# Two key and bias buffers in attention, four-token gate one-hots and another hand-over order in a hybrid transformer block

## The chip, the cores and the metric

The kernel runs on one core of one Trainium2 chip. The metric is device time in microseconds of one launch. The profiled execution is one further launch with the hardware profiler on.

## The reference

One layer on x of 1024 tokens by 1024 features, in f32:

```
mod = silu(c) @ w_ada + b_ada                  # shift, scale, gate for both halves
h = rms_norm(x) * (1 + scale1) + shift1
proj = h @ w_in
  heads A (8 x 64): attention of each 64-token chunk on itself and 8 chunks before it,
                    q and k normed, a learned bias by clipped distance, softmax
  heads B (4 x 128): short causal conv on q, k, v, then the chunked gated delta rule
x = x + gate1 * (concat(A, B) @ w_out)
h2 = rms_norm(x) * (1 + scale2) + shift2
PEER: q = h2 @ w_query; for each of 8 heads top 16 of 128 x 128 product keys
      y = sum_k gate_k * gelu(u_k . h2) * v_k   # u, v rows of expert_down, expert_up (16384 x 1024)
out = x + gate2 * y
```

## The kernel before, in words

The tokens are 8 tiles of 128 and are worked on in the groups [0], [1, 2], [3, 4], [5, 6], [7]. All work up to the expert stage is written as generators, each called under a lane name (lines 1056 to 1074):

- P, `project` (lines 395 to 507): norm, all input projections of a group; the results go to the DRAM tensor `rec` by kind and tile.
- D, `delta` (589 to 664): the delta rule of one tile, with a state that goes from tile to tile. Its tiles come from a ring of 12 buffers of 128 x 512 f32.
- M, `attention` (510 to 569): one tile, one head pair after the other (four pairs). For a pair, `kv` (line 516) receives the queries (line 517) and five tiles of keys and of values (line 519), and `near` (line 521) the bias of the two nearest tiles. Scores (line 532) go to PSUM, VectorE adds the bias and takes the extreme (line 536), ScalarE takes the exponential (539), TensorE transposes (548) and multiplies with the values (556). `kv` and `near` have one buffer each and the lane has one PSUM bank.
- O, `output` (688 to 755): output projection, residual, second norm and the query product with its top 16, for a group.
- R, `choose` (767 to 846): the top 16 of the candidates and the softmax weights of a tile.
- G, `gates_dense` (851 to 885), for tiles 2 to 5: it spreads the 128 weights of each token over the 128 x 128 experts. For 8 tokens at a time (`GQ`, line 66), VectorE makes two one-hot tiles of 128 x 1024 in f16 (line 870); for each token ScalarE scales the second of them twice, by a high and a low part (line 877), and TensorE multiplies it with the first (line 878). Four tokens fill a PSUM bank, which ScalarE empties into `stg` (line 881); 16 tokens of `stg` are stored to `gd`. The one-hot and scaled tiles come from a ring of six buffers, and the lane has one PSUM bank, that of R.

Tiles 0, 1, 6 and 7 take the sparse path instead: `down` and `up` (894 to 930) gather 128 rows of 4 KB per token slot through GpSimd's queue, and VectorE works on them. Those of tile 0 and the down part of tile 1 are issued in the front; the others stand beside the dense stage. The dense stage (932 to 1031) runs tiles 2 to 5 against all 16384 experts; its buffers take the place of those of the lanes, which are released ahead of it (line 1075).

The order of the instructions on each engine is fixed when the program is built. A planner runs through all of them and, on each engine, takes the ready instruction with the lowest priority number; a buffer is taken when one of its ring is free. The numbers come from the lane and the tile alone: `when` (line 1053) gives tile number x 10000 plus the lane's constant in `PRI`, `lane` (line 141) sets it, and each instruction counts it on. So for tile t, delta rule and attention come before output, projections of later tiles and gates:

```
PRI = {'P': -2000, 'D': -15000, 'M': -16000, 'O': -5000, 'R': 0, 'G': 5000, 'A': 60000, 'U': 59000, 'C': 2000000}
```

PSUM tiles of a lane come from its own banks (`BANKS`: P 2, D 2, M 1, O 2, R 1), unless `SPREAD` names several lanes for a tile; then `mm` (line 151) takes their banks in turn.

Of the kernel before, what the change touches and what calls it, by code (L numbers as in the profile page):

```python
# [30 lines left out]
P = 128  # L31
# [17 lines left out]
NROW = 3  # L49
NMORE = 4  # L50
NHELD = 2
RINGS = {'P': 4, 'D': 12, 'M': 4, 'O': 3, 'R': 2, 'G': 6}
XBUFS = {'P': 1, 'O': 2}
WBUFS = {'P': 4, 'O': 3}
STEP = 10000
PRI = {'P': -2000, 'D': -15000, 'M': -16000, 'O': -5000, 'R': 0, 'G': 5000, 'A': 60000, 'U': 59000, 'C': 2000000}
SPREAD = {('P', 0): 'PR', ('D', 0): 'DDO'}
LAYOUT = 'acc more upp rawp wd dn hc gp'
DBUFS = dict(acc=1, more=NMORE, wd=SCN + 1, upp=SCN, hc=1, gp=3, dn=2, rawp=3)
FIRST = {'P': 1000, 'D': 1000, 'M': 1000, 'O': 1000, 'R': 1000, 'G': 1000}  # L60
# [2 lines left out]
SHIFT = {}  # L63
SLOPE = {}
BANKS = dict(P=2, D=2, M=1, O=2, R=1)
GQ = 8
GROUPS = [[0], [1, 2], [3, 4], [5, 6], [7]]
STARTS = [0, 16, 24] + [32 + 4 * k for k in range(5)] + [52 + k for k in range(8)]
LEVELS = (1, 2, 4, 8, 16, 32, 64)
# [49 lines left out]
def hybrid_layer(ctx, tc, a, out):  # L119
# [36 lines left out]
    def lt(shape, dt, name, bufs, tag=None):  # L156
        return pools_[cur[0][0]].tile(list(shape), dt, name=name, tag=(tag or name) + cur[0], bufs=bufs)
# [352 lines left out]
    def attention(t, mixT):  # L510
        m0 = max(0, 4 - t)
        nk = 5 - m0
        oa = rg()
        for p in range(4):
            cs = slice(p * P, (p + 1) * P)
            kv = lt([P, 11, P], F, "kv", 1)
            SP.dma_start(kv[:, 0, :], rec[QA, t][:, cs])
            for n, kind in ((1, KA), (6, VA)):
                SP.dma_start(kv[:, n + m0:n + 5, :],
                             rec[kind, t - 4 + m0:t + 1, :, cs].rearrange("m p c -> p m c"))  # L520
            near = lt([P, 2, 256], F, "near", 1)
            SP.dma_start(near, neard[:, 2 * p:2 * p + 2])
            ss_, rs = [], sm(2)
            for hh in range(2):
                hp = slice(hh * 64, hh * 64 + 64)
                s = lt([P, 640], F, "sx", 2)
                init = BIG
                for lo, hi, bias in ((m0, 3, farm[:, min(m0, 2) * P:]), (max(m0, 3), 5, near[:, hh, (max(m0, 3) - 3) * P:])):
                    if lo >= hi:
                        continue  # L530
                    ps = mm()
                    PE.matmul(ps[:, :(hi - lo) * P], kv[hp, 0, :],
                              kv[hp, 1 + lo:1 + hi, :].rearrange("p m c -> p (m c)"), start=True, stop=True,
                              skip_group_check=True)
                    mf = sm(1)
                    V.tensor_tensor_reduce(s[:, lo * P:hi * P], ps[:, :(hi - lo) * P], bias, -1.0, init, OP.add,
                                           OP.min, accum_out=mf)
                    init = mf
                A_.activation(s[:, m0 * P:], s[:, m0 * P:], AF.Exp, bias=mf, scale=-1.0, accum_out=rs[:, hh:hh + 1])
                ss_.append(s)  # L540
            yield
            blocks = [(hh, m) for hh in range(2) for m in range(m0, 5)]
            PT = {}
            for b0 in range(0, len(blocks), 4):
                part = blocks[b0:b0 + 4]
                pt = mm()
                for n, (hh, m) in enumerate(part):
                    PE.transpose(pt[:, n * P:(n + 1) * P], ss_[hh][:, m * P:(m + 1) * P], ident)
                d = rg()
                A_.activation(d[:, :len(part) * P], pt[:, :len(part) * P], AF.Copy)  # L550
                for n, bm in enumerate(part):
                    PT[bm] = d[:, n * P:(n + 1) * P]
            po = mm()
            for hh in range(2):
                for m in range(m0, 5):
                    PE.matmul(po[:, hh * 64:hh * 64 + 64], PT[hh, m], kv[:, 6 + m, hh * 64:hh * 64 + 64],
                              start=(m == m0), stop=(m == 4), skip_group_check=True)
            V.reciprocal(rs, rs)
            V.tensor_tensor(v3(oa[:, cs], 2), v3(po[:, 0:P], 2), b3(rs, AD), OP.mult)
            yield  # L560
        junk = rg()
        ss = sm(1)
        A_.activation(junk, oa, AF.Square, accum_out=ss)
        r = rsqrt(ss, 1, 1.0 / 512)
        A_.activation(oa, oa, AF.Copy, scale=r)
        ps = transpose4(oa)
        for j in range(4):
            A_.activation(mixT[:, j, :], ps[:, j * P:(j + 1) * P], AF.Copy, scale=mixg[:, j:j + 1])
        yield
# [281 lines left out]
    def gates_dense(t):  # L851
# [11 lines left out]
        V.tensor_tensor(parts[:, 1, :], parts[:, 0, :], ghalf, OP.subtract)  # L863
        for blk in range(8):
            stg = lt([P, P, 16], F, "stg", 1)
            for q in range(2):
                n0 = blk * 16 + q * GQ
                oh1, oh2, whi, wlo = (rg((P, GQ * P), BF).rearrange("p (n i) -> p n i", n=GQ) for _ in range(4))
                for oh, key in ((oh1, 0), (oh2, 1)):
# [184 lines left out]
        return max(FIRST.get(name, 1000), t * SLOPE.get(name, STEP) + PRI[name] + SHIFT.get((name, t), 0))  # L1054

    tc.cur_priority = 0
    for n, g in enumerate(GROUPS):
        lane("P", when("P", g[0]), run, project(g), tile_=g[0])
        if n == 0:
            with tc.issue_after(first_loads):  # L1060
                lane("M", NEARP, run, near_bias())
            lane("P", ADAP, run, ada_rest())
        mixT = pools_["O"].tile([P, KD, 256], F, name="mixT", tag="mixT", bufs=1)
        for tt, t in enumerate(g):
            own = mixT[:, :, tt * P:(tt + 1) * P]
# [29 lines left out]
```

## Time and profile before

| what | value |
|---|---|
| runs | 3506.4, 3490.28, 3504.95 us; median 3504.95 us |
| profiled execution | 3495.83 us, span of its instructions 3494.1 us |
| mean granted TensorE clock | 0.902 |
| TensorE busy (matmul) | 3014.0 us, 86% |
| VectorE busy | 2719.5 us, 78% |
| ScalarE busy | 1316.2 us, 38% |
| GpSimd busy | 1310.2 us, 37% |
| HBM | 282 GB/s over the span |

Shares are of the span of the profiled execution. PE is TensorE, DVE VectorE, ACT ScalarE, POOL GpSimd, SP the engine whose queue issues nearly all other transfers. A row such as "DVE x <- PE y" is idle time of the first engine that a signal of the second ended. Since the kernel has two parts with different work, the averages over the span say little; the stretches have to be read one by one.

### The profile page before, as it was taken

Reading aid. Unit: us, or ns where it says so; the run is one execution under the profiler, and the core shown is the slowest. Engines: PE = TensorE matmul, PEld = TensorE weight load, DVE = VectorE, ACT = ScalarE, POOL = GpSimd, SP = SyncE. Lnnn points to the kernel's source line nnn. Section 1 sums busy time; section 2 is a strip of 40 time slices with the busy share of each in tenths; the row PEclk is TensorE's granted clock in tenths of the full one; section 3 lists DMA queues with packets and bytes.
Section 4 is the critical chain, followed back from the end, with each engine's and each line's share of the span. In section 5 each row is a group of like instructions: output and inputs, shape, how many; then the busy total and the mean of one; then the engine's idle time right before and its main releaser. Section 6 shows DMA issues by size and latency. Waiting matters only on the chain.

```text
span 3494.1 us, 44943 instructions
## 1 busy us (share of the span) xinstructions
PE 3014.0 (86%) x15196; PEld 2482.1 (71%) x15196; DVE 2719.5 (78%) x6407; ACT 1316.2 (38%) x2833; POOL 1310.2 (37%) x1028
## 2 busy tenths in 40 slices
PE   7988868798887898576877699999999999999998
PEld 5677756677766787465756577877777777777777
DVE  3347668768899778993585888988888888889898
ACT  2333134233235663386767632222222222222222
POOL 0000333432333323430000155556655556655563
PEclk9988878899878899686878899999999999999999
DMA  8865888898777987773435699999999999999997
GB/s 283 284 215 174 274 282 267 270 336 280 261 250 230 354 297 261 258 250 125 157 119 176 218 345 334 344 341 339 328 330 336 344 337 349 335 333 355 344 332 283
DMA packets 375959, 989.71 MB, mean 283 GB/s; under 512 B 33440, under 2 KB 139296, under 8 KB 375728
## 3 DMA queue, kind: packets, MB, share of 16 engines
q0 software_dynamic: 147456, 536.94, 43.4%
q1 hardware_dynamic: 228272, 449.90, 37.6%
q8 instruction: 119, 1.95, 0.2%
q14 instruction: 112, 0.92, 0.1%
HBM read 924.84 MB, written 61.87 MB: 282 GB/s over the span
## 4 chain that ended last, share of the span: by engine, by line
PE 37%; DMA 26%; DVE 20%; issue 9%; ACT 5%; POOL 3%; SPq 0%; DVEq 0%; POOLq 0%; ACTq 0%
PE at L982 12%; DMA row<-in_peer_expert_down_dram,idx 8%; PE yk L1005 6%; PE mm L365 5%; PE yc L1005 4%; DVE row L903 4%; DMA row<-in_peer_expert_up_dram,idx 4%; DMA rawu<-in_peer_expert_up_dram 4%; DVE y L920 4%; PE mm L351 3%; DMA rawd<-_peer_expert_down_t_dram 2%; POOL row L901 2%; DMA g<-gd 2%; ACT rg L877 2%; DMA w<-in_w_ada_dram 1%
## 5 line engine op out<-in xcount | busy, mean ns | idle before, releaser
L901 POOL DMA_INDIRECT row<-in_peer_expert_down_dram,idx x512 | 645.5, 1261 | 1113.0 <-DVE s L310 353.7
L915 POOL DMA_INDIRECT row<-in_peer_expert_up_dram,idx x512 | 664.5, 1298 | 1035.5 <-DMA g<-gd 421.3
L903 DVE CUSTOM_DVE_ANT_0 row<-row,h2a 128x1024 f32<-128x1024 f32 x512 | 619.7, 1222 | 139.4 <-DMA row<-in_peer_expert_down_dram,idx 138.6
L920 DVE SCALAR_TENSOR_TENSOR y<-row,act,y 128x1024 f32<-128x1024 f32 x508 | 651.8, 1283 | 53.3 <-DMA row<-in_peer_expert_up_dram,idx 50.1
L877 ACT ACTIVATE rg<-rg,gparts 128x128 f16<-128x128 f16 x1024 | 318.3, 396 | 75.7 <-PE mm L878 49.0
L985 ACT ACTIVATE gl<-at 128x512 f32<-128x512 f32 x128 | 76.4, 597 | 670.8 <-PE at L982 670.8
L982 PE MATMUL at<-hhi,dhi 128*128 128x512 f32 x1024 | 260.6, 396 | 16.3 <-ACT dhi L963 16.2
L365 PE MATMUL mm<-h2T,w 128*128 128x256 f32 (+1 forms) x1280 | 251.8, 358 | 19.0 <-DMA w<-in_peer_w_query_dram 8.2
L982 PE MATMUL at<-hlo,dhi 128*128 128x512 f32 x1024 | 256.8, 392 | 0.0
L1005 PE MATMUL yk<-uhi,whi 128*128 128x512 f32 x512 | 202.5, 412 | 61.7 <-ACT whi L991 56.4
L351 PE MATMUL mm<-w,hT 128*128 128x256 f32 x1024 | 249.3, 398 | 7.3 <-DMA w<-in_w_in_dram 4.6
L982 PE MATMUL at<-hhi,dlo 128*128 128x512 f32 x1024 | 254.7, 389 | 0.7 <-DVE dlo L964 0.7
L365 PEld LDWEIGHTS mm<-h2T,w 128*128 128x128 f32 x1280 | 218.2, 205 | 44.7 <-DMA w<-in_peer_w_query_dram 9.7
L982 PEld LDWEIGHTS at<-hhi,dhi 128*128 128x128 f32 x1024 | 194.7, 191 | 60.1 <-ACT dhi L963 19.0
L351 PEld LDWEIGHTS mm<-w,hT 128*128 128x128 f32 x1024 | 199.2, 200 | 45.3 <-DMA w<-in_w_in_dram 6.4
L982 PEld LDWEIGHTS at<-hlo,dhi 128*128 128x128 f32 x1024 | 194.4, 190 | 41.0
L982 PEld LDWEIGHTS at<-hhi,dlo 128*128 128x128 f32 x1024 | 192.2, 188 | 41.0 <-DVE dlo L964 1.2
L1005 PE MATMUL yk<-ulo,whi 128*128 128x512 f32 x512 | 204.0, 404 | 3.5 <-DVE ulo L964 3.5
L1005 PE MATMUL yc<-uhi,whi 128*128 128x512 f32 x512 | 205.1, 401 | 0.5 <-DVE yacc L1014 0.5
L1005 PE MATMUL yc<-ulo,whi 128*128 128x512 f32 x512 | 204.2, 399 | 0.0
L1005 PE MATMUL yc<-uhi,wlo 128*128 128x512 f32 x512 | 199.5, 390 | 0.0
L870 DVE TENSOR_TENSOR rg<-iota_n,gkeys 128x1024 f16<-128x1024 f16 x128 | 151.0, 1222 | 55.9 <-PE mm L878 55.8
(300 smaller groups left out, 5582.1 us busy)
## 6 DMA issues: line engine op xcount, KB each, us to landing
w<-in_w_in_dram SPq DMA_DIRECT2D x140, 512.0 KB
rawd<-_peer_expert_down_t_dram SPq DMA_DIRECT2D x128, 512.0 KB
rawu<-in_peer_expert_up_dram SPq DMA_DIRECT2D x128, 512.0 KB
w<-in_peer_w_query_dram SPq DMA_DIRECT2D x80, 512.0 KB
gd<-stg SPq DMA_DIRECT2D x64, 512.0 KB
g<-gd SPq DMA_DIRECT2D x32, 1024.0 KB
w<-in_w_ada_dram SPq DMA_DIRECT2D x48, 512.0 KB
w<-in_w_out_dram SPq DMA_DIRECT2D x40, 512.0 KB
```

The source lines that it names most:

```text
L351: PE.matmul(ps[t][:, hf * 256:hf * 256 + 256], hT[:, k, tt * P:(tt + 1) * P], w[k], start=(k == 0), stop=(k == KD - 1), skip_group_check=True)
L365: PE.matmul(ps[:, (c % per) * W:(c % per + 1) * W], w[k][:, (c % 2) * P:(c % 2 + 1) * P], hT[:, k, :W], start=(k == 0), stop=(k == KD - 1) ...
L870: V.tensor_tensor(oh, iota_n[:, None, :].to_broadcast([P, GQ, P]), keys[:, key, n0:n0 + GQ, None].to_broadcast([P, GQ, P]), OP.is_equal)
L877: A_.activation(w[:, n, :], oh2[:, n, :], AF.Copy, scale=parts[:, m, n0 + n:n0 + n + 1])
L901: G.indirect_dma_start(out=r, out_offset=None, in_=a["peer_expert_down"], in_offset=bass.IndirectOffsetOnAxis(ap=idx[:, j:j + 1], axis=0))
L903: V.tensor_tensor_reduce(r, r, h2, 1.0, 0.0, OP.mult, OP.add, accum_out=act[:, j:j + 1])
L915: G.indirect_dma_start(out=row, out_offset=None, in_=a["peer_expert_up"], in_offset=bass.IndirectOffsetOnAxis(ap=idx[:, j:j + 1], axis=0))
L920: V.scalar_tensor_tensor(y, row, w[:, j:j + 1], y, op0=OP.mult, op1=OP.add)
L982: PE.matmul(ps, l[:, k, :], r[:, k, :], start=(n == 0), stop=(n == 3 * KD - 1))
L985: A_.activation(g, ps, AF.Gelu)
L1005: PE.matmul(ps, l[:, ts_], r[:, cs], start=(m == 0 and (s == 0 or not own)), stop=(m == 3 * SCN - 1 and (s == NK // SCN - 1 or not own)))
```

## The change

Five edits. `kv` and `near` of attention get two buffers each. The gates work on 4 tokens at a time, so that a one-hot tile is 128 x 512 and there are four quarters in a block of 16 tokens in place of two halves. The delta rule's ring has 11 buffers. Tile 5's gates take PSUM banks of lanes G (one) and P (two) in turn. The projections of group n + 1 are handed over before the delta rule, attention, output and routing of group n, instead of after them.

```diff
-RINGS = {'P': 4, 'D': 12, 'M': 4, 'O': 3, 'R': 2, 'G': 6}
+RINGS = {'P': 4, 'D': 11, 'M': 4, 'O': 3, 'R': 2, 'G': 6}
...
-SPREAD = {('P', 0): 'PR', ('D', 0): 'DDO'}
+SPREAD = {('P', 0): 'PR', ('D', 0): 'DDO', ('G', 5): 'GP'}
...
-GQ = 8
+GQ = 4
...
-            kv = lt([P, 11, P], F, "kv", 1)
+            kv = lt([P, 11, P], F, "kv", 2)
...
-            near = lt([P, 2, 256], F, "near", 1)
+            near = lt([P, 2, 256], F, "near", 2)
...
-            for q in range(2):
+            for q in range(16 // GQ):
...
-    for n, g in enumerate(GROUPS):
+    def projections(n):
+        g = GROUPS[n]
         lane("P", when("P", g[0]), run, project(g), tile_=g[0])
         if n == 0:
             with tc.issue_after(first_loads):
                 lane("M", NEARP, run, near_bias())
             lane("P", ADAP, run, ada_rest())
+
+    projections(0)
+    for n, g in enumerate(GROUPS):
+        if n + 1 < len(GROUPS):
+            projections(n + 1)
         mixT = pools_["O"].tile([P, KD, 256], F, name="mixT", tag="mixT", bufs=1)
```

## Rows read from the trace of the kernel before

**Rows 1.** The page, TensorE's busy tenths and granted clock in 40 slices of the span.

```profile
PE   7988868798887898576877699999999999999998
PEclk9988878899878899686878899999999999999999
```

**Rows 2.** Busy time by stretch: start:end, length, engines, granted clock, DMA share, GB/s.

```profile
0.00:1965.00 1965.00, 1576.46 (x9042) 1311.04 (x9043) 1387.51 (x4671) 904.57 (x2308) 440.99 (x394) 0.85 0.72 244
1965.00:3494.00 1529.00, 1437.55 (x6157) 1171.08 (x6155) 1332.03 (x1737) 411.63 (x527) 869.17 (x634) 0.98 0.93 334
1200.00:1580.00 380.00, 293.00 (x1807) 249.68 (x1805) 328.28 (x1116) 215.51 (x572) 126.57 (x106) 0.84 0.80 271
1580.00:1640.00 60.00, 35.27 (x170) 25.43 (x171) 23.78 (x58) 42.73 (x126) 0.00 (x0) 0.51 0.33 108
1640.00:1838.00 198.00, 164.96 (x936) 135.55 (x935) 130.01 (x621) 134.62 (x394) 0.00 (x0) 0.81 0.42 140
```

**Rows 3.** Timeline of TensorE where the dense stage begins: start us, us, line, operation.

```profile
1936.90 0.44 PE L365 MATMUL mm<-h2T,w 128*128 128x128 f32 x2
...
1964.50 1.01 PE L878 MATMUL mm<-rg 128*128 128x128 f16 x8 [2.48 <-ACT stg L881]
1967.20 3.55 PE L982 MATMUL at<-hhi,dhi 128*128 128x512 f32 x8 [1.69 <-ACT dhi L963]
```

**Rows 4.** Ends of lanes by line (first and last start), and one from ScalarE's timeline.

```profile
L568 ACT ACTIVATE mixT<-mm,mix_gain x32: 347/361/386, 182.7 to 1837.6; 128x128 f32<-128x128 f32 x32
...
1638.51 1.11 ACT L568 ACTIVATE mixT<-mm,mix_gain 128x128 f32<-128x128 f32 x4
...
L663 ACT ACTIVATE mixT<-mm,mix_gain x8: 687/687/738, 180.2 to 1666.7; 128x512 f32<-128x512 f32 x8
...
L837 DVE TENSOR_TENSOR gd<-gd,s x4: 277/296/303, 1051.6 to 1811.8; 128x128 f32<-128x128 f32 x4
...
L881 ACT ACTIVATE stg<-mm x32: 575/597/620, 1635.7 to 1803.6; 128x512 f32<-128x512 f32 x32
...
L858 DVE CAST gkeys<-mm x4: 417/426/427, 1090.1 to 1822.2; 128x256 f16<-128x256 f32 x4
```

**Rows 5.** Timeline of TensorE, first and last seam between two head pairs of attention.

```profile
1217.64 1.91 PE L556 MATMUL mm<-kv,rg 128*128 128x64 f32 x8
...
1231.36 0.91 PE L532 MATMUL mm<-kv 64*128 64x384 f32 x2
...
1791.75 2.13 PE L556 MATMUL mm<-kv,rg 128*128 128x64 f32 x9
...
1797.80 1.62 PE L532 MATMUL mm<-kv 64*128 64x384 f32 x2 [1.37 <-DMA kv<-rec]
```

**Rows 6.** Waits of SP's queue in the front: us, times, longest.

```profile
SPq L517 <- PE mm L556: 127.7, 26, 13.1
...
SPq L522 <- DVE s L536: 93.2, 21, 20.0
```

**Rows 7.** VectorE's groups in the front: count, busy us, mean ns, idle before.

```profile
L870 DVE TENSOR_TENSOR rg<-iota_n,gkeys 128x1024 f16<-128x1024 f16 x128 | 151.0, 1222 | 55.9 <-PE mm L878 55.8
...
L632 DVE TENSOR_TENSOR rg<-rg,mm 128x512 f32<-128x512 f32 x40 | 27.3, 683 | 11.0 <-PE mm L630 10.9
...
L820 DVE TENSOR_TENSOR rg<-rg 128x512 f16<-128x512 f16 x28 | 11.3, 426 | 0.0
```

**Rows 8.** Waits from 1461 to 1975 us, gates of tiles 3 to 5.

```profile
DVE rg L870 <- PE mm L878: 50.5, 20, 7.6
...
ACT rg L877 <- PE mm L878: 31.7, 19, 4.9
...
ACT rg L877 <- DVE rg L870: 20.0, 7, 5.8
```

**Rows 9.** Waits from 1822 to 1975 us, gates of tile 5.

```profile
PE mm L878 <- ACT stg L881: 30.3, 12, 6.4
...
DVE rg L870 <- PE mm L878: 25.2, 7, 7.6
```

## The prediction

> **What bounds the kernel now.** I read the page's slices first: TensorE's digits are 9s only in the second part of the span, and in the first part both they and the granted clock are uneven [rows 1]. The table by stretches puts numbers to it: up to 1965 us (the front: projections, delta rule, attention, output, routing, gates) TensorE is busy 1576 of 1965 us at a granted 0.85, from there to the end (the dense expert stage) 1438 of 1529 us at 0.98 [rows 2]. The diff touches nothing in the dense stage, so I leave its 1529 us alone and ask only when it can start. The timeline around 1965 us shows that: tile 7's last query matmuls end at 1937, tile 5's gates still run at 1965 and the first dense matmul starts at 1967 [rows 3]. Two chains thus reach the same point: output of tile 7, which needs attention of tile 7, and gates of tile 5, which need output and routing of group [5, 6].
>
> The ends of the lanes say which lane is behind both. Attention of tile 7 ends at 1838 while the delta rule of that tile has been done since 1667; attention of tile 6 ends at 1639, the output of [5, 6] starts there, routing of tile 5 is done at 1812, and tile 5's gate keys are taken at 1822, after the last evacuation of tile 4's gates at 1804 [rows 4]. So attention is the late lane, by 170 us over the delta rule, and the gate lane comes second.
>
> **Attention's second buffers.** The tile `kv` holds queries, keys and values of one head pair, and with one buffer the loads of the next pair cannot be issued until the last value matmul of this one. From tile 5's second pair to tile 7's fourth there are eleven such seams. From the end of the last value matmul to the next first score matmul they last 11.8 us (the first, 1219.6 to 1231.4), then 17.3, 15.4, 48.1, 5.3, 8.8, 3.8, 21.9, 4.1, 9.7 and 3.9 us (the last, 1793.9 to 1797.8) [rows 5]: 150.1 us in all, 110.5 us in the seven ahead of the output of [5, 6]. The queue that issues the loads shows the same from its side: SP stood 127.7 us, 26 times, in front of the query load for the value matmul, and 93.2 us in front of `near` for the pass over the scores [rows 6]. Both waits go; the 128 loads of attention (32 of queries, 64 of keys and values, 32 of `near`) then stand earlier in SP's order than the weight loads that queued behind them. What they come to wait for next is the projection's stores of keys and values, unchanged by the diff.
>
> How much of 110.5 us is gained? Not all: TensorE did other lanes' work in the seams. From 1200 to 1838 us it was busy 293.0 + 35.3 + 165.0 = 493.3 of 638 us, so 22.7% idle [rows 2]. If only idle time can be filled, the gain is 0.227 x 110.5 = 25 us; if attention simply goes first and the other work finds room elsewhere, 110 us (150 us for tile 7's chain). Work of attention has to be finished before output, routing and gates can be, while most of what ran in the seams does not, so I take half, **55 us**, and keep 25 and 150 for the range.
>
> **Gate one-hots of four tokens.** The 128 VectorE operations of 1024 columns become 256 of 512; ScalarE's and TensorE's counts stay, with as many evacuations and stores. The price of a 512-column operation on this operand is not in the trace. The present one takes 1222 ns for 1024, one element a cycle as for f32; an f32 operation of 512 columns takes 683 ns, the 16-bit fold of 512 columns in routing 426 ns [rows 7]. I take the f32 row, since both it and the present form run at the slow rate: 256 x 0.683 - 151.0 = 24 us more VectorE time over four tiles. By the fold's row it would be 42 us less, which is the other end. The Trainium skill (VectorE: DVE Perf Modes, The perf-mode tier table) says that a 16-bit `tensor_tensor` in SBUF runs at twice the rate; that is the fold's price, and the sum would be 42 us less VectorE time. The trace does not bear it out for this operation, whose 1222 ns is the single rate, one operand being a key repeated along the columns. VectorE was busy 130.0 of 198 us from 1640 to 1838 us [rows 2], so this is covered where ScalarE has one-hots in hand; ScalarE waited for them 20.0 us from 1461 us to the end of the front [rows 8]. I charge a quarter of that, **+5 us**.
>
> The ring keeps six buffers, now of half the size, and a quarter still needs four. So the point where ScalarE's second scaled one-hot must wait for TensorE's last matmul of the quarter before comes every four tokens instead of every eight. ScalarE waited so 31.7 us from 1461 to 1975 us [rows 8]; doubled that is +32 us, and 0 if each wait halves. I take a third, **+11 us**. VectorE's own wait in that ring, 50.5 us, should come twice as often and half as long; I take 0, with -25 and +50 as ends.
>
> **Three banks for tile 5's gates.** In that tile's stretch TensorE waited 30.3 us for ScalarE to empty the one bank, and VectorE 25.2 us for those matmuls to give ring buffers back [rows 9]. With three banks in turn, two of them left idle by the projections, a block's matmuls no longer wait for the evacuation before. At most 30 us, at least 0 (ScalarE's own work for a block remains and may set the pace alone); I take half, **-15 us**.
>
> **The rest at nothing.** The delta rule's ring goes from 12 to 11 buffers: a load or a transpose waits for the next free one. Its cover is the 170 us by which this lane is ahead at tile 7 [rows 4]; if attention gained all 150 us, that cover would shrink to 20 us. Handing the next group's projections over first changes no priority number: `when` works it out from lane and tile, and `where` carries it on, whatever the order of the calls. I count 0, and no more than a few us either way from ties. It adds no DMA and moves none past POOL's.
>
> **Sum.** -55 + 5 + 11 - 15 = -54 us. The profiled execution took 3495.83 us (span 3494.1), so 3442 us. The median of the runs shown is 9.1 us above it, where the same saving reads 3451; I give 3446.
>
> **Rivals.** First, **one bank keeps attention in series**: the lane's PSUM bank (M=1) is not doubled, and every score, transpose and value product of a pair passes through it. Then the second `kv` saves only what the load itself takes, while the gates' +16 and -15 us cancel. For it: the eleven seams are 150 of the 618 us from the first of them to the end of tile 7's attention; three quarters of a pair's time lie inside the pair, where the bank is held. Against it: SP's 127.7 us were waits for the buffer, not the bank. Time about 3496, within 0.5% of before (I call 17 us, 0.5% of the median, the least that a measurement of this kernel can tell from no change). The Trainium skill (Perfetto Trace Analysis, Matmuls) asks that independent groups rotate through several banks; by it the gates' change pays and attention's does not.
>
> Second, **the gate ring decides**, on the slow side: gates of tiles 3, 4 and 5 follow one another from 1461 to 1974 us, so this lane too reaches the end of the front. If both ring waits double (+31.7 and +50.5 us), with +5 for the one-hots, and attention yields only its 25 us, no bank gain left, the result is 3495.8 + 62 = 3558 us; with half the doubling it is 3495.8 + 41 + 5 - 25 = 3517 us. It decides as soon as the ring's growth passes what attention and banks give, 25 to 70 us. For it: VectorE's 50.5 us is the longest wait on an engine there that serves every lane. Against it: a half-size quarter also frees its buffers in half the time.
>
> Third, **all seams close**: -150 + 1 = 3347 us, with the other work moved into TensorE's idle time and its clock higher for it. For it: the front's granted 0.85 beside 0.98 later [rows 2]. Against: VectorE was 86% busy from 1200 to 1580 us, which attention needs too.
>
> **How the numbers follow.** The forecast, attention's seams closing in part, gets 0.53, with its own range 3380 to 3487. All seams 0.12, one bank 0.17, the gate ring 0.18. Faster by over 0.5% (under 3487): 0.53 + 0.12 = 0.65; within 0.5%: 0.17; slower: 0.18. The range runs from 3360 to 3530: it leaves out most of the third rival and the upper half of the second.
>
> **What would show it.** In the profile after: SP's waits for the value matmul and for `near` gone or below a third; seams of 2 to 4 us; attention of tile 7 ending some 50 us before 1838, the first dense matmul near 1913, and the dense stage still 1529 us long. The one-hot operations should be 256 of about 0.68 us, and TensorE's wait for the evacuation in tile 5's stretch below 15 us. I am wrong if attention ends where it did (bank), if gates of tiles 3 and 4 take over 170 us each (ring), if the dense stage changes its length by more than 15 us, or if the delta rule ends behind attention.

## The result, and the profile after

The changed kernel takes 3470.75 us (median of 6 runs, 3465.62 to 3477.73), the kernel before 3501.63 us in the same session (6 runs); the ratio is 0.9927 with the 95% interval 0.9902 to 0.9952. So it is faster by 31 us by the medians and by 26 us by the ratio, where 59 were forecast (3504.95 for the kernel before, 3446 for the changed one). Two runs below had one slow execution each (4358.66 us at a granted clock of 0.63, 5008.53 at 0.55), and their medians are of the five others. The profiled execution of the changed kernel took 3471.64 us with a span of 3469.9.

The page's slices, TensorE's busy tenths and granted clock, against [rows 1]:

```profile
PE   7887788799888998688967999998999999999998
PEclk9998878899878998688958999999999999999999
```

The nines begin one slice earlier than in [rows 1], and an 8 stands among them where there was none. The table by stretches (start:end, length, TensorE, weight loads, VectorE, ScalarE, GpSimd, granted clock, DMA share, GB/s) gives the sizes, against [rows 2]:

```profile
0.00:1923.00 1923.00, 1580.15 (x9053) 1297.53 (x9054) 1407.43 (x4844) 912.08 (x2314) 421.15 (x394) 0.86 0.73 250
1923.00:3469.90 1546.90, 1442.78 (x6144) 1174.80 (x6144) 1319.37 (x1693) 407.26 (x517) 873.06 (x634) 0.97 0.91 329
1574.00:1777.00 203.00, 168.06 (x998) 138.75 (x998) 140.45 (x653) 157.17 (x458) 0.00 (x0) 0.81 0.42 147
```

The front holds the same TensorE work (1580 us busy, 1576 before) in 42 us less. The dense stage has 18 us more, at 329 instead of 334 GB/s and a clock 0.01 lower. From the first dense matmul (1922.7, 1967.2 before) to the end of the span it is 1547 us long instead of 1527. So the front gives 44 us and the dense stage takes 20 back. These are one profiled execution each. In the three later runs that change the kernel before behind its front alone, the first dense matmul is at 1952 to 1979; in the five that do so to the changed kernel, at 1920 to 1931.

TensorE's timeline where the dense stage begins, against [rows 3], now runs from tile 5's last gate matmul straight into it:

```profile
1921.47 0.58 PE L878 MATMUL mm<-rg 128*128 128x128 f16 x2 [0.48 <-ACT rg L877]
1922.74 3.47 PE L982 MATMUL at<-hhi,dhi 128*128 128x512 f32 x8 [0.69 <-ACT stg L881]
```

The ends of the lanes (shortest, median and longest ns, first and last start), against [rows 4]:

```profile
L568 ACT ACTIVATE mixT<-mm,mix_gain x32: 348/368/379, 177.7 to 1778.1; 128x128 f32<-128x128 f32 x32
L663 ACT ACTIVATE mixT<-mm,mix_gain x8: 680/687/703, 181.5 to 1604.7; 128x512 f32<-128x512 f32 x8
L837 DVE TENSOR_TENSOR gd<-gd,s x4: 279/282/283, 1030.6 to 1751.6; 128x128 f32<-128x128 f32 x4
L858 DVE CAST gkeys<-mm x4: 407/417/426, 1065.1 to 1788.0; 128x256 f16<-128x256 f32 x4
```

Attention ends 59.5 us earlier (1837.6 to 1778.1), the delta rule 62, routing of tile 5 60, and tile 5's gates begin 34 us earlier. All lanes moved together, and attention stayed the late one.

The first seam of [rows 5], at tile 5's second head pair, now reads:

```profile
1195.00 4.32 PE L556 MATMUL mm<-kv,rg 128*128 128x64 f32 x20
1201.82 1.02 PE L532 MATMUL mm<-kv 64*128 64x384 f32 x2
```

The seam is 2.5 us (11.8 before). Of the eleven, nine are 2.5, 3.8, 6.8, 3.5, 2.4, 12.1, 1.3, 8.8 and 1.3 us, 42.5 in all where they were 80.1. The two at the start of a tile stay, 43.5 us (48.1) and 23.1 us (21.9): there attention waits for something other than the buffer. Half of the gain came earlier than I had counted: tile 5's second pair starts 30 us earlier already (1201.8, 1231.4 before). SP's waits of the front, against [rows 6], did not go and did not fall below a third:

```profile
SPq L517 <- PE mm L556: 103.0, 20, 13.9
...
SPq L522 <- DVE s L536: 51.9, 13, 18.4
```

SP still waits, since two pairs are loaded ahead and the third stands where the second stood; but the wait now lies a pair ahead of its use.

The gates. VectorE's one-hots as the page groups them (busy us, mean ns, idle before), against [rows 7]; then the waits from 1455 to 1925 us against [rows 8], and of tile 5's gates alone, 1788 to 1925 us, against [rows 9]:

```profile
L870 DVE TENSOR_TENSOR rg<-iota_n,gkeys 128x512 f16<-128x512 f16 x256 | 164.9, 685 | 74.8 <-PE mm L878 69.3
```

```profile
DVE rg L870 <- PE mm L878: 58.3, 26, 8.3
ACT rg L877 <- PE mm L878: 39.7, 22, 6.6
...
ACT rg L877 <- DVE rg L870: 23.6, 26, 3.2
```

```profile
DVE rg L870 <- PE mm L878: 28.5, 12, 5.5
PE mm L878 <- ACT rg L877: 18.5, 23, 2.7
PE mm L878 <- ACT stg L881: 4.3, 2, 3.0
```

256 one-hots of 685 ns (683 forecast); the ring's two waits grew by 7.8 and 8.0 us; TensorE's wait for the evacuation fell from 30.3 to 4.3 us, and in its place it waits 18.5 us for ScalarE's one-hots. From the cast of a tile's keys (L858) to the end of its last evacuation (L881), the gates of tiles 3, 4 and 5 take 184, 154 and 135 us, where they took 165, 177 and 152: tile 3 is over the 170 that the forecast named as the sign of the ring, tile 4 is not, and the sum falls.

Last the dense stage, which the forecast did not look at. TensorE's waits there, in the kernel before from 1965 us and in the changed one from 1923 us (us, times, longest; `at` is the first product with the expert weights, `yk` the second):

```profile
PE yk L1005 <- ACT whi L991: 56.4, 27, 5.2
PE at L982 <- ACT dhi L963: 16.2, 7, 3.4
PE yk L1005 <- ACT uhi L963: 5.0, 3, 2.1
```

```profile
PE yk L1005 <- ACT whi L991: 60.2, 23, 5.3
PE at L982 <- ACT dhi L963: 30.9, 9, 6.7
PE yk L1005 <- ACT uhi L963: 2.3, 5, 1.2
```

All gaps between the stage's matmuls add up to 81 us before and 95 after, and the matmuls themselves take 1437 and 1443 us for the same work. These 14 + 6 are the 20 us. TensorE is the busiest engine of this stage and waits for ScalarE, which splits the expert weights (`dhi`) and the gated tile (`whi`) into two parts.

### The profile page after: what moved, and what is told of

Its sections match the earlier page's. It is cut to its first block, busy times and chain, and to the rows that moved or that the text cites. A ratio compares the mean times of both kernels' runs of the same rounds, so it can differ in the third digit from the quotient of the medians.

```text
span 3469.9 us, 45183 instructions
## 1 busy us (share of the span) xinstructions
PE 3022.9 (87%) x15196; PEld 2472.3 (71%) x15196; DVE 2726.8 (79%) x6535; ACT 1319.3 (38%) x2830; POOL 1294.2 (37%) x1028
## 4 chain that ended last, share of the span: by engine, by line
PE 26%; issue 8%; DMA 7%; POOL 5%; DVE 5%; ACT 3%; POOLq 0%; ACTq 0%; SPq 0%; DVEq 0%
PE at L982 11%; PE yk L1005 5%; PE yc L1005 4%; POOL row L915 3%; DMA rawu<-in_peer_expert_up_dram 3%; POOL row L901 2%; PE mm L365 2%; DMA rawd<-_peer_expert_down_t_dram 2%; ACT rg L877 1%; PE mm L351 1%; DVE row L903 1%; DVE rg L870 1%; DMA row<-in_peer_expert_up_dram,idx 1%; DMA row<-in_peer_expert_down_dram,idx 1%; DMA gd<-stg 1%
## 5 line engine op out<-in xcount | busy, mean ns | idle before, releaser
L915 POOL DMA_INDIRECT row<-in_peer_expert_up_dram,idx x512 | 652.3, 1274 | 1085.0 <-issue 431.1
L877 ACT ACTIVATE rg<-rg,gparts 128x128 f16<-128x128 f16 x1024 | 329.5, 395 | 105.7 <-PE mm L878 57.0
L365 PEld LDWEIGHTS mm<-h2T,w 128*128 128x128 f32 x1280 | 211.1, 198 | 31.4 <-DMA w<-in_peer_w_query_dram 8.4
L870 DVE TENSOR_TENSOR rg<-iota_n,gkeys 128x512 f16<-128x512 f16 x256 | 164.9, 685 | 74.8 <-PE mm L878 69.3
```

The costliest lines, as they stand in the source:

```text
L365: PE.matmul(ps[:, (c % per) * W:(c % per + 1) * W], w[k][:, (c % 2) * P:(c % 2 + 1) * P], hT[:, k, :W], start=(k == 0), stop=(k == KD - 1) ...
L870: V.tensor_tensor(oh, iota_n[:, None, :].to_broadcast([P, GQ, P]), keys[:, key, n0:n0 + GQ, None].to_broadcast([P, GQ, P]), OP.is_equal)
L877: A_.activation(w[:, n, :], oh2[:, n, :], AF.Copy, scale=parts[:, m, n0 + n:n0 + n + 1])
L915: G.indirect_dma_start(out=row, out_offset=None, in_=a["peer_expert_up"], in_offset=bass.IndirectOffsetOnAxis(ap=idx[:, j:j + 1], axis=0))
```

## Experiments

All are compared with runs of the kernel before on the same chip; medians and ratios with 95% intervals. "Gaps" are TensorE's between the first dense matmul and the last, from the profiled execution.

**Four parts of the change.** The hand-over alone, put into the kernel before, leaves every engine's instructions in the same order, so it was not run; two pairs of key and bias buffers without four-token one-hots do not fit in SBUF, nor does the delta rule's ring of 12 beside them, so neither was run alone.

```
-            kv = lt([P, 11, P], F, "kv", 2)
-            near = lt([P, 2, 256], F, "near", 2)
+            kv = lt([P, 11, P], F, "kv", 1)
+            near = lt([P, 2, 256], F, "near", 1)
```

> The changed kernel with one buffer each for kv and near again; the four-token one-hots, the 11-buffer ring, the hand-over order and tile 5's three banks stay. Theory A (the gain of the front is attention's seams): attention of tile 7 ends again at 1825 to 1850 us, the first dense matmul comes at 1955 to 1975, and the time is 3490 to 3515 us. Rival B (the gain is the gates' three banks): the first dense matmul stays at 1925 to 1940 and the time at 3470 to 3485 us.

Measured: 3480.41 us, 0.9961 (0.9940 to 0.9982). Attention ends at 1823.6 and the first dense matmul is at 1956, 33 us after that of the changed kernel, yet only 10 us of this show in the time, which lies under the 3490 to 3515 us that were expected: gaps 70 us instead of 95. The second pair does what it should in front, and the dense stage hides it.

```
-SPREAD = {('P', 0): 'PR', ('D', 0): 'DDO', ('G', 5): 'GP'}
+SPREAD = {('P', 0): 'PR', ('D', 0): 'DDO'}
```

> The changed kernel with tile 5's gates on the one bank of their lane again; all else stays. Theory A: attention of tile 7 still ends near 1777 us, TensorE waits 25 to 35 us for the evacuation in tile 5's stretch, the first dense matmul comes 5 to 20 us later than 1923. Rival B: 30 us or more later. Apart from that the dense stage is asked: if its 1547 us in the changed kernel (1527 before) come from the order in which the gathers of the sparse tiles are interleaved there, which this edit puts back to the pattern of before, it lasts 1520 to 1530 us here and the total is about 3470; if they come from the one-hots, the ring or an earlier start, it lasts 1540 to 1550.

Measured: 3458.62 us, 0.9879 (0.9851 to 0.9907), 12 us faster than the changed kernel. But tile 5's gates are slower with the one bank: they take 147 us instead of 135, their last evacuation is at 1949 instead of 1922 (15 of these 27 us are there when their keys come, at 1803 instead of 1788), and expert tile 8, counted from 0, starts at 2024 instead of 2003. The first dense matmul is at 1920, 3 us earlier and not 5 to 20 later as expected: the stage starts while the gates still run. TensorE's wait for the evacuation in these gates (1802 to 1950 us) is back at 25 us:

```profile
PE mm L878 <- ACT stg L881: 25.0, 15, 4.1
```

So with the banks expert tile 8 comes 20 us earlier, 12 of them in tile 5's gates, and the dense stage takes more than that away again: 1323 us from expert tile 8 to tile 120 here, 1359 in the changed kernel, 1329 in the kernel before. (From the first dense matmul to the end it is 1538 us, neither of the two lengths that were expected.) From here on the question was what makes this stretch longer.

```
-    projections(0)
     for n, g in enumerate(GROUPS):
-        if n + 1 < len(GROUPS):
-            projections(n + 1)
+        projections(n)
```

> The changed kernel with the projections handed over in the old order, group by group. Theory C (the order of the calls matters only where two lanes share banks: tile 7's projections then come behind tile 5's gates in the projections' two banks): tile 7's projections end later than 1600 us instead of 1542, attention of tile 7 ends 30 us or more later than 1777, and the time is 3500 us or more. Rival D (priority numbers alone decide, as the prediction has it): the same time as the changed kernel, 3465 to 3480 us.

Measured: 3637.42 us, 1.0404 (1.0378 to 1.0430). The step that I priced at nothing is worth 167 us here. The last of the projections' decay line (L432), of the gates' keys (L858) and of attention (L568), first and last start at the end of each row:

```profile
L432 DVE TENSOR_TENSOR bgall<-s,na x8: 149/158/161, 54.2 to 1824.4; 128x4 f32<-128x4 f32 x8
...
L858 DVE CAST gkeys<-mm x4: 414/417/425, 1062.0 to 1719.2; 128x256 f16<-128x256 f32 x4
...
L568 ACT ACTIVATE mixT<-mm,mix_gain x32: 345/366/377, 171.8 to 1983.4; 128x128 f32<-128x128 f32 x32
```

Tile 5's gates take banks of the projections now. Buffers of a bank go round in the order in which the program asks for them, and with the old order tile 5's gates ask before tile 7's projections do. So tile 7's projections, which in the changed kernel are through that line before 1300 us, stand behind tile 5's gates, whose keys come at 1719: the line ends at 1824 and tile 7's attention at 1983. The new hand-over is what makes the three banks possible.

```
-GQ = 8
+GQ = 4
-            for q in range(2):
+            for q in range(16 // GQ):
```

(in the kernel before)

> The kernel before with four-token one-hots alone (one kv and near, 12 buffers, old order, one bank). Theory A with the prediction's price: 24 us more VectorE time (256 of about 685 ns), ring waits about as before, time 0 to 20 us longer, 3500 to 3522 us. Rival E (the ring decides): gates of tiles 3 and 4 take over 170 us each and the time is 3530 us or more. Rival F (the smaller one-hots let TensorE and ScalarE start sooner): 10 to 30 us shorter, 3472 to 3492 us.

Measured: 3488.11 us, 0.9978 (0.9959 to 0.9997), 4 us faster in the median of 12 runs (8 by the ratio) and so close to nothing; +16 was forecast for the one-hots and the ring. The first dense matmul is 11 us earlier here (1956) and the gaps are 83 us.

**Is it the order of the gathers?** The rows of tiles 6 and 7 are gathered during the dense stage. In the kernel before and in the run with one bank, up rows of tile 6 and down rows of tile 7 alternate one by one but for seven or eight pairs; in the changed kernel about half of the groups are pairs and threes. That was the first theory. The edit puts each gather behind the one issued before it (the chain):

```
+    def gather(**kw):
+        with tc.issue_after(gathered[0]) if gathered else ExitStack():
+            i = G.indirect_dma_start(**kw)
+        if keep_order[0]:
+            gathered[:] = [i.ins]
...
-            G.indirect_dma_start(out=r, out_offset=None, in_=a["peer_expert_down"],
+            gather(out=r, out_offset=None, in_=a["peer_expert_down"],
...
+    keep_order[0] = True
     experts(LATE)
```

> The changed kernel with one edit: among the expert tiles handed over last, every gather of expert rows (down rows of one token tile, up rows of the next) is ordered behind the gather that the program issues before it, so that the two kinds alternate one by one as in the kernel before. Theory 'gather order' (the planner emits them in pairs and threes in the changed kernel, and that costs the dense stage): the stretch from the 8th to the 120th expert tile falls from 1359 us back to 1317 to 1340, the attention's end and the first dense matmul stay at about 1777 and 1923, and the time is 3440 to 3455. Rival 'something else in the dense stage' (another start, another place of the buffers in SBUF, the ring of 11): the stretch stays at 1350 to 1365 and the time at 3465 to 3478. Third possibility: the chain itself holds gathers back that could have gone, and the stretch is longer than 1365.

Measured: 3462.26 us, 0.9902 (0.9874 to 0.9931). The stretch fell to 1320 us as the theory had it, gaps 79 us, but the gain is 8 us, within the two intervals; the end behind the last matmul is 23 us long, 9 without the chain.

The same chain with two steps of a lane per turn, in the run with one bank and in the kernel before:

```
-                    if lane(*item, live) is live:
-                        live.remove(item)
+                    for _ in range(2 if len(live) > 1 else 1):
+                        if lane(*item, live) is live:
+                            live.remove(item)
+                            break
```

> The changed kernel with tile 5's gates on one bank again (3458.6 us, stretch from the 8th to the 120th expert tile 1323 us), and the gathers of the expert tiles handed over last forced into pairs: two down tiles, then two up tiles. Theory 'gather order': the stretch grows by 15 to 40 us and the time is 3472 to 3500. Rival 'something else': no more than 5 us, 3455 to 3464.

> The kernel before with the gathers forced into pairs in the same way, nothing else. Theory 'gather order': its stretch from the 8th to the 120th expert tile grows from 1329 to 1344 to 1370 us and its time by 15 to 40 us, to 3507 to 3532. Rival 'something else': within 5 us of the kernel before. If the pairs cost in one of the two kernels and not in the other, the order matters only together with where the dense stage starts.

Measured: 3472.04 us, 0.9922 (0.9896 to 0.9948), 13 us more than without, and 3518.93 us, 1.0061 (1.0040 to 1.0082), 22 us more. That looked like the theory, but the stretches did not grow as it asked: 1326 us (1323 without) and 1335 (1329). In both, 12 of the microseconds lie behind the last matmul.

```
+    projections(1)
     for n, g in enumerate(GROUPS):
-        if n + 1 < len(GROUPS):
-            projections(n + 1)
+        if n + 2 < len(GROUPS):
+            projections(n + 2)
```

(and `('G', 4): 'GP'` beside `('G', 5): 'GP'`)

> The changed kernel with the projections handed over two groups ahead instead of one, and tiles 4 and 5 both with three banks for their gates; with this the gathers come out one by one in turn. Theory 'gather order': the dense stretch is 1317 to 1340 us; tile 4's gates and tile 5's gates end earlier, the first dense matmul is at 1905 to 1925, and the time is 3430 to 3455, under both kernels. Rival 'shared banks': the gates of tile 4 now share two banks with the projections of tile 7, and the first dense matmul is at 1930 or later, with a time of 3455 to 3475.

Measured: 3462.64 us, 0.9900 (0.9873 to 0.9927). The front is the shortest of all with three weight buffers, first dense matmul at 1907; the gathers alternate one by one as in the kernel before; and the stretch is 1357 us with gaps of 104 us, more than with any forced pairs. That contradicts the theory.

> The kernel with the projections handed over two groups ahead (3462.6 us, TensorE's waits in the dense stage 104 us, stretch from the 8th to the 120th expert tile 1357 us), with the gathers of the expert tiles handed over last ordered one behind the other. They come out one by one in turn there without that too, so the order of the kinds is hardly changed. Theory 'gather order' in its strict form (only pairs and threes cost): no change, 3457 to 3468, stretch 1350 to 1362. Rival 'how far the gathers run ahead of the expert tiles' (the chain holds them to the program's own pace; up to 13 more were done by the 96th tile than in the kernel before): TensorE's waits fall to 70 to 90 us, the stretch to 1320 to 1335, the time to 3435 to 3450. Rival 'earlier start' (a stage that starts earlier is longer, whatever the order): stretch 1350 or more, time 3457 or more.

> A control: the kernel before with its gathers ordered one behind the other, which is nearly the order that it has. Every theory of the order: 3487 to 3507, TensorE's waits in the dense stage 70 to 90 us (81 before). If it is more than 10 us slower, the chain itself has a price, which then is to be taken off the runs that use it.

Measured: the same with the chain 3454.47 us, 0.9877 (0.9856 to 0.9897), stretch 1336, gaps 91, a gain of 8 us that lies between what was expected, with intervals that overlap; the kernel before with the chain 3520.56 us, 1.0054 (1.0036 to 1.0073). The control decides: chaining the gathers in nearly the order that they have anyway costs the kernel before 19 us by the ratio, about as much as forcing pairs did (21). Half of it is the end, where TensorE has nothing left (last stretch of that run, span 3523.7):

```profile
3505.00:3524.00 19.00, 0.00 (x0) 0.00 (x0) 10.10 (x13) 0.00 (x0) 0.00 (x0) 0.55 0.54 193
```

In the kernels up to here without a chain this end is 8.8 us. So the pairs were not shown to cost by themselves, and gaps of 95 us (this control) and 104 us (two groups ahead) come with no pairs or few. What all these runs share is that the gaps go with the stage's length: 70, 79, 81, 83, 86, 87, 89, 91, 95, 95, 99 and 104 us in the twelve kernels up to here, for 1506 to 1547 us from the first dense matmul to the last, with no part of the change that explains the order.

**Weights that land late.** ScalarE waits for the transfers of the first kind of expert weights (`rawd`; in the kernel before, then in the changed one), and three buffers hold both kinds:

```profile
ACT dhi L963 <- DMA rawd<-_peer_expert_down_t_dram: 66.8, 23, 7.1
```

```profile
ACT dhi L963 <- DMA rawd<-_peer_expert_down_t_dram: 84.4, 19, 10.0
```

One buffer of gathered rows has the size of one weight buffer:

```
-NMORE = 4
+NMORE = 3
-DBUFS = dict(acc=1, more=NMORE, wd=SCN + 1, upp=SCN, hc=1, gp=3, dn=2, rawp=3)
+DBUFS = dict(acc=1, more=NMORE, wd=SCN + 1, upp=SCN, hc=1, gp=3, dn=2, rawp=4)
```

> The changed kernel with one buffer less for gathered rows in the dense stage and one more for expert weights, of the same size. Theory 'weights land late' (in the changed kernel TensorE waits 31 us for the split of down weights, 16 us in the kernel before, and ScalarE 84 against 67 us for the weights' transfer, since more gathers are in flight ahead of it): the wait for the down weights falls under 16 us, TensorE's waits in the dense stage from 95 to 65 to 80 us, the time to 3445 to 3460. Rival 'VectorE' (the waits come from gathered rows that VectorE takes ahead of the dense stage's own work): no change in the wait of the second product for the gated tile (60 us), the time 3463 to 3480; with one buffer less the gathers may fall behind and the time rise.

> The changed kernel with tile 5's gates on one bank (3458.6 us; TensorE's waits in the dense stage 87 us, 14 of them for down weights) and the same exchange of a row buffer for a weight buffer. Theory 'weights land late': little to gain, 3448 to 3460. Rival 'VectorE': 3455 to 3470.

Measured: 3421.40 us, 0.9777 (0.9755 to 0.9800), gaps 3 us, far under what the theory asked; with one bank for tile 5's gates 3432.01 us, 0.9817 (0.9794 to 0.9840), gaps 16 us. The order of the two has turned round: with the gaps gone, three banks are 11 us better by the medians (14 with 11 either way by the ratios), not 12 worse. Where these come from is not shown: the last dense matmul ends 3 us later with three banks in the profiled executions, what follows it is 8 us shorter, and their times differ by 5.5 us. The second run gained 27 us where the theory had 10 at most; I had taken the waits for `dhi` alone, and the 59 us for `whi` went with them.

The edit changes two things, so they were taken apart. In the kernel before and the changed one, a fourth weight buffer alone (both keep all row buffers); in the changed one, a row buffer less alone, and five weight buffers:

```
-DBUFS = dict(acc=1, more=NMORE, wd=SCN + 1, upp=SCN, hc=1, gp=3, dn=2, rawp=3)
+DBUFS = dict(acc=1, more=NMORE, wd=SCN + 1, upp=SCN, hc=1, gp=3, dn=2, rawp=4)
```

> The kernel before with a fourth buffer for expert weights in the dense stage, nothing else. Theory 'weights land late' (the changed kernel loses some 20 us of its 44 to 48 us in front because TensorE waits more often for weights, and that loss has nothing to do with what the change does in front): TensorE's waits in the dense stage fall from 81 to under 20 us, the granted clock there is 1.00, and the kernel before with four buffers is slower than the changed kernel with four by the whole front's gain, 40 to 50 us: 3455 to 3480 if the changed one is at 3415 to 3435. Rival 'an earlier start costs by itself' (the transfers left over set the end): the two come closer, with a difference of 25 us or less.

> The changed kernel with a fourth buffer for expert weights, and the gathered rows' buffers kept (one of them was given up in the run with four weight buffers, 3421 us). Theory 'weights land late': TensorE's waits in the dense stage at most 15 us, time 3400 to 3425. Rival 'too many gathers in flight' (it was the buffer taken from the gathers that helped): waits of 60 us or more, 3440 to 3470.

> The changed kernel with one buffer less for gathered rows and three weight buffers as it has. Theory 'weights land late' for want of a buffer: TensorE's waits stay over 60 us and the time at 3460 or above. Rival 'too many gathers in flight': waits under 30 us, time 3415 to 3440.

> The changed kernel with five buffers for expert weights. Once TensorE no longer waits, the transfers set the end: within 8 us of the run with four buffers and all row buffers. If it is more than 10 us faster, four buffers still leave weights late; if more than 10 us slower, weights fetched further ahead hold the gathers back, which then end last.

Measured: kernel before with four 3466.45 us, 0.9905 (0.9882 to 0.9927); changed kernel with four 3413.33 us, 0.9754 (0.9729 to 0.9779); with one row buffer less 3434.89 us, 0.9814 (0.9790 to 0.9838); with five 3409.28 us, 0.9734 (0.9712 to 0.9756). The middle of the dense stage, 2100 to 3300 us, in that order before, after, before with four, after with four, one row buffer less (columns as in the table by stretches above):

```profile
2100.00:3300.00 1200.00, 1135.92 (x4860) 927.15 (x4861) 1043.22 (x1388) 318.45 (x405) 711.08 (x517) 0.98 0.94 339
```

```profile
2100.00:3300.00 1200.00, 1113.94 (x4723) 904.96 (x4722) 1014.19 (x1356) 312.19 (x395) 690.56 (x500) 0.97 0.92 330
```

```profile
2100.00:3300.00 1200.00, 1197.60 (x5284) 991.67 (x5283) 1062.15 (x1433) 348.86 (x445) 699.09 (x504) 1.00 0.96 344
```

```profile
2100.00:3300.00 1200.00, 1199.68 (x5292) 992.90 (x5291) 1062.24 (x1430) 350.62 (x445) 698.39 (x504) 1.00 0.95 343
```

```profile
2100.00:3300.00 1200.00, 1185.40 (x5201) 976.26 (x5201) 1045.03 (x1410) 344.28 (x434) 680.62 (x496) 1.00 0.94 338
```

With three weight buffers the two kernels do different amounts in the same 1200 us (4860 and 4723 matmuls); with four they do the same (5284 and 5292), with gaps of 4 and 3 us in the whole stage, at a granted clock of 1.00. ScalarE's wait for `rawd` goes with them, here in the changed kernel with four:

```profile
ACT dhi L963 <- DMA rawd<-_peer_expert_down_t_dram: 8.2, 3, 7.4
```

And then the change is worth 53 us of the medians (ratios 0.9905 and 0.9754, apart by 0.0151 with about 0.0034 either way, 53 us with 12 either way): the gain of the front arrives, within that error. The rival, that an earlier start costs by itself, allowed 25 us and falls by the medians. The two profiled executions are 35 us apart, with 25 us between their first dense matmuls (1951.5 and 1926.5); the one of the kernel before is the fastest of its six, 18 us under their median. A row buffer less does most of it too (gaps 18 us), which the theory in its strict form, the want of a buffer, did not allow; the rival there, too many gathers in flight, had it within its range. So either remedy takes TensorE's waits away. In that run the down rows of tile 7 are gathered with 43 pairs among them, as in the changed kernel (42 pairs and threes), and the gaps are small: pairs alone do not make them. A fifth buffer adds nothing that can be told (0.9734 and 0.9754). In these kernels the gathers end last: the last matmul ends 83 to 93 us before the span does, and what is left runs at 365 GB/s (changed kernel with four, first row). So in them the front's gain reaches the end not through TensorE but through GpSimd's gathers. The rows of up gathers (kernel before with four, then changed kernel with four) show the first one of the dense stage 47 us earlier and the last one 35 us earlier:

```profile
3330.00:3411.00 81.00, 0.00 (x0) 0.00 (x0) 73.36 (x62) 0.00 (x0) 43.43 (x43) 0.50 0.95 365
```

```profile
L915 POOL DMA_INDIRECT row<-in_peer_expert_up_dram,idx x378: 932/1142/4549, 1976.9 to 3420.2; - x189
```

```profile
L915 POOL DMA_INDIRECT row<-in_peer_expert_up_dram,idx x378: 932/1149/3802, 1929.4 to 3385.2; - x189
```

**The second pair once more, and a candidate.** The changed kernel with four weight buffers and one pair (edit of the first run and the one above), and the kernel with two groups handed over ahead with five weight buffers:

> The changed kernel with four weight buffers (3413 us) and one key and one bias buffer in attention instead of two. With TensorE not waiting in the dense stage, the second pair's own worth can be read without the dense stage's scatter. The forecast's term for it was 55 us (ends 25 and 110), the run with one pair and three weight buffers had its first dense matmul 33 us later than the changed kernel. Theory 'the front's gain arrives whole': 3440 to 3455. Rival 'an earlier start costs by itself': 3428 or less.

> A candidate that may beat all others: projections handed over two groups ahead, tiles 4 and 5 with three banks for their gates, five weight buffers (with one group ahead and tile 5 alone 3409 us). Its front had the first dense matmul at 1907, 16 us before the changed kernel. Theory 'the front's gain arrives whole': 3390 to 3402. Rival 'transfers set the end': 3405 or above.

Measured: 3458.10 us, 0.9891 (0.9869 to 0.9913), so the second pair is worth 45 us (3458.10 - 3413.33; 0.0137 of the ratio with 0.0033 either way, 48 us with 12). I expected 3455 at most and missed by 3 us. The candidate takes 3400.08 us, 0.9720 (0.9698 to 0.9742), the lowest of the study and within what was expected, 9 us under the kernel with five buffers and one group ahead, though the intervals overlap; its first dense matmul was at 1919 this time, 12 us before that one's, so the 16 us did not stay 16.

## Why the prediction was right or wrong

**Attention (-55).** Right in mechanism and near in size, the size in part by luck. The end of its lane moved by 59.5 us, and where the dense stage lets it through the second pair is worth 45 us. Two points in it were off: SP's waits do not go, they move a pair ahead (103.0 of 127.7 and 51.9 of 93.2 us are left); and I counted the seams from tile 5 on, while 30 us of the gain are made before that. The seven seams that the 55 us were taken from shrank by 36 us (110.5 to 74.4). The first rival, one bank that keeps attention in series, is refuted by the row of L568, and the third, that all seams close, by the seams: 41 of the 150 us went.

**One-hots (+5) and ring (+11).** VectorE's price was read from the right row: 685 ns, 256 x 685 - 128 x 1222 = 19 us more. The Trainium skill's tier table (VectorE: DVE Perf Modes, The perf-mode tier table) gives a 16-bit `tensor_tensor` in SBUF twice the rate; this form, with a key repeated along the columns, does not show it at 685 ns, beside the fold's 426. The ring's waits grew by 16 us together (8.0 for ScalarE, where 11 were charged, and 7.8 for VectorE, where 0 was), not to the double. Together with the three banks, the hand-over and the D ring they give nothing that can be told: the changed kernel with one pair and four weight buffers is at 3458.10 us (0.9891), the kernel before with four at 3466.45 us (0.9905), and the intervals overlap; forecast was +1 for them all. The gate ring as the bound, the rival on the slow side, is refuted.

**Three banks (-15).** Near: the wait fell from 30.3 to 4.3 us, 18.5 us of waiting for ScalarE's one-hots came in its place, which the term had allowed for, and tile 5's gates are 12 us shorter than with one bank (9 with four weight buffers, 139 against 148). By itself, that is, with the old hand-over, the part costs 167 us.

**Hand-over (0).** That it changes no priority number was true and not enough. Alone it leaves the order of the instructions as it was, but it decides in which order the shared banks are taken. I looked at each line of the diff by itself and not at the two together.

**The dense stage: the step that failed.** "The diff touches nothing in the dense stage, so I leave its 1529 us alone." Its code is the same, its time is not: 20 us longer, which is what turned 44 us of gain in front (10 less than the sum) into 24 in the profiled executions. The text named a change of more than 15 us there as what would prove it wrong, and that is what came. The views for it had been there: TensorE stood 81 us in this stage at a clock of 0.98, waiting for ScalarE, with transfers at 0.93 of the DMA engines' time, and the twelve kernels with three weight buffers and all row buffers had gaps of 70 to 104 us there. With a fourth weight buffer the waits are gone in both kernels and the change brings 53 us (12 either way), against 54 forecast by the sum. That the two agree so closely is in part luck: in those kernels the gathers end last, and not the stage's matmuls, whose start was all that the forecast asked for.

**Left open.** Why the changed kernel's interleaving is 14 us worse than that of the kernel before, and not better as with one pair of buffers (70 us of gaps). The order of the kinds of gathers does not explain it, nor does an earlier start by itself; twelve kernels scatter between 70 and 104 us and no single edit explains them. Each figure is from one execution, so how much of the scatter is between executions of one kernel is not known either. Nor is it told apart whether the fourth buffer works through the transfers alone or also through the order that the planner then chooses: with one row buffer less ScalarE still waits 97.3 us for `rawd`, more than in the changed kernel, and TensorE hardly waits, so late weights alone do not settle when TensorE waits:

```profile
ACT dhi L963 <- DMA rawd<-_peer_expert_down_t_dram: 97.3, 40, 10.6
```

## What to carry to other kernels

Before a saving in one stage is passed on to the end, read the waits of the stage that follows: where its bound engine waits for transfers with few buffers, its length need not be a constant; here 20 us came with the change, and 34 us lay between the least and the greatest gaps. A buffer more at that place made the other edits readable here, and it was worth more than the change itself (57 us in the changed kernel, 35 in the kernel before). Where an edit lets two kinds of work share banks, the order in which the program asks for them is part of the edit.

## What the runs showed that was not expected

Waits of 81 us in a stage of 1518 us went with more than themselves: where they are gone, the granted clock there is 1.00 (that of 2.4 GHz) in place of 0.98, the same matmuls take 1397 instead of 1437 us, and the matmuls' part of the stage shrinks by 116 us (1518 to 1402, kernel before without and with the fourth buffer). The time falls by only 35 us of it, and the gathers then end last. One buffer of gathered rows less makes the kernel 36 us faster, although GpSimd's gathers are what ends last in it.
